# The multiplications of a level half a step after its exponentials, in the recurrence of a two-block kernel

## The chip, the cores and the metric

One NeuronCore of a Trainium2 chip runs the whole program. The time is device microseconds of one execution; before the change three runs gave 2949.8, 2950.39 and 2955.82 us, median 2950.39. The engines are named as the profile names them: PE (TensorE, matrix products; PEld its weight loads), DVE (VectorE), ACT (ScalarE), POOL (GpSimd), SP (SyncE, which here only issues DMAs). Each engine works off its own instructions strictly in order; semaphores make one wait for another.

## What is computed

Two transformer blocks on 512 latent tokens of 1024 features. The change lies in the first block, in a gated linear recurrence (HGRN) with eight heads of 128 features, run forwards and backwards over the tokens. For one direction and chunks of 128 tokens it is

```
def step(s, blk):
    qc, lfc, kc, vc = blk
    b = jnp.cumsum(lfc, axis=2)
    decay = jnp.exp(jnp.where(lower, b[:, :, :, None, :] - b[:, :, None, :, :], -jnp.inf))
    a = jnp.einsum('bhtd,bhsd,bhtsd->bhts', qc, kc, decay)
    o = jnp.einsum('bhts,bhse->bhte', a, vc) + jnp.einsum('bhtd,bhde->bhte', qc * jnp.exp(b), s)
    b_last = b[:, :, -1:, :]
    s_new = jnp.exp(b_last)[:, :, 0, :, None] * s + jnp.einsum('bhsd,bhse->bhde', kc * jnp.exp(b_last - b), vc)
    return s_new, o
```

`log_f` and `k` are the logarithms of a sigmoid of one projection and of its complement. The outputs of both directions are added, normed over the 128 features (`o * rsqrt(mean(o*o) + eps)`), scaled and multiplied with `silu` of another projection. The rest of the block (a gated convolution, grouped attention, a merge, sixteen experts) and the second block are the same before and after.

## The kernel before

Features stand on the partitions, tokens along the free dimension. For each head j a generator `mixer_in` (L628) makes eight products of the 512 latents with a slab of 128 weight columns, four of them with the context's 256 tokens too, and what follows from them alone: the gates of both directions (`lf`, `az`, running sums `P`), the query `q`, the output gate `g`, the values `v` and the convolution `cv`, `b`. A product is 24 matmuls (three for each of 8 k tiles, since each operand is split into two float32r parts) or 48. ACT makes the high part of a weight slab (`whi<-raw`, L153), POOL the low part (`wlo<-raw,whi`, L110), eight of each for a head.

A second generator `hgrn_core` (L738) does the recurrence of the head before. The decays between two tokens of a chunk are taken by halves: for each level m in 16, 8, 4, 2, 1 and 32, 64, the tokens of a block of 2m are decayed to its middle. `halves(m)` (L801) writes four differences of the running sums `P` into a tile `dd` of [128, 2, 512] on DVE, and ACT takes the exponential of all of it; then DVE multiplies its first half with the keys `k` and the second with `q`. PE then forms the products of keys and queries: `near(m)` for levels up to 16, `far(m)` for 32 and 64, and DVE and ACT copy what belongs to the level into `a` or `aT`. The states of the chunks are a chain: PE forms `u` from the turned, decayed keys `kt` and the values, ACT copies the first state `S<-u`, and DVE does three `S<-S,eq,u` for each direction. `read` (L855) makes the output `o` and ACT its squares `sq`; `norm` (L865) sums them over the features on PE (`hs`), then ACT takes Ln and Exp and DVE does four operations on `rstd` and `rstd_t` and multiplies `o` with the result to `a`, which SP stores. Both `o` and `hs` lie in the two PSUM banks that `near` and `far` use as well.

The order is written out by hand. `mixers` (L891) runs the generators side by side: of the eight products of a head each is followed by half a step of the recurrence, what frees the product's bank, another half step, and the rest. A head's recurrence begins with the first product of the next head and, in its last four half steps, goes along with the recurrence of the head after it. Since every engine is in order, the place of an instruction in this program decides what it queues behind. Products take PSUM banks in turn, `dd` has three buffers. After the last head the same loop runs with the keys and values of the attention (`attn_kv`, L963) in the place of projections.

Of the kernel before, what the change touches and what calls it, by code (L numbers as in the profile page):

```python
# [20 lines left out]
S = 512  # L21
# [11 lines left out]
def shape_constants():  # L33
    """Tables that follow from the shapes alone."""
# [33 lines left out]
class Flow:  # L68
    """Slabs of 128 weight columns in the order in which the products use them: loads and exact
    splits into two float32r parts run ahead of the products."""  # L70
# [43 lines left out]
    def fill(self, parts=True):  # L114
        """Loads go out as far ahead as there is room; splits follow a call later, so that no
        engine waits for them."""
        n, there = len(self.plan), self.loaded
        more = True
        while more:
            more = False  # L120
            if self.parted < self.loaded and (self.parted < there or self.parted <= self.pos):
                if len(self.parts) < (self.nparts if parts is True else parts):
                    self.part()
                    more = True
            if self.loaded < n and self.loaded - self.parted < self.nraw:
                self.load()
                more = True
# [10 lines left out]
class Kernel:  # L138
# [42 lines left out]
    def banks(self, es, mm, **pools):  # L181
        """PSUM pools of a phase: mm banks for products, the others by name (tiles, banks each)."""
# [14 lines left out]
    def lin(self, slab, outs):  # L197
        """outs: (psum, high parts, low parts) with one [128, n] part for each k tile."""
# [9 lines left out]
    def first_constants(self, pin):  # L208
# [27 lines left out]
        # resets of the running sums: every 128, every 32, at the start  # L236
# [8 lines left out]
    def first_tables(self):  # L245
        """What the shapes give and the start needs."""
# [24 lines left out]
    def vectors(self, pin, name, items):  # L271
        """Vectors of features, brought to [128, n / 128] with the features on the partitions."""
# [47 lines left out]
    def conditions(self, conds):  # L320
        """silu of c, c_ctx and c_2, features on the partitions, in 32 columns for each 128 features"""
# [5 lines left out]
    def first_mods(self, pool, bufs):  # L327
        """Shifts and scales of the first modulation for c, c_ctx and c_2 at once, 128 features of
        both in a step: functions for the load, the products, and the sums over the partitions."""
# [30 lines left out]
    def mod_load(self, pool, tag, bufs, queue):  # L360
        """The next pair of slabs of the modulations."""
# [6 lines left out]
    def modulate(self, pool, n, bufs, bank, cuts=1, late=1):  # L368
        """Modulations of the one condition that is needed, n pairs of slabs: the products on VectorE
        and only the sums over the partitions on TensorE. Returns a function for a step: the  # L370
        products of a pair take as many calls as there are cuts, and with one buffer the load one
        more. late: how many pairs later the sums come."""
# [47 lines left out]
    def gain(self, name, g, mods, chunk, col):  # L420
        """g * (1 + scale) as [128, 8]."""
# [5 lines left out]
    def rstd(self, pool, ps, n=S, tag="rstd", bufs=2):  # L427
        """ps holds -0.5 * mean of squares, the same in all partitions that share a group."""
# [4 lines left out]
    def rstd_in(self, y, t, ps, eps=None):  # L433
        col, eps = (self.eps2, EPS * EPS) if eps else (self.eps, EPS)
        self.act(y, ps, AF.Ln, scale=-2.0, bias=col)
        self.act(y, y, AF.Exp, scale=-0.5)
        self.tt(t, y, y, OP.mult)
# [14 lines left out]
    def tokens_norm(self, pool):  # L452
        """Two tiles of tokens at a time, as they come."""
# [30 lines left out]
    def tokens_turned(self, k, pool, P):  # L484
        """features k on the partitions, latents and context side by side"""
# [9 lines left out]
    def split(self, pool, src, n=S, tag="h", bufs=None, e=("act", "pool")):  # L495
        """Exact float32r parts of src."""
# [7 lines left out]
    def tokens_modulated(self, k, xn, ph, phc, pool):  # L504
        """h of the latents and of the context, features k, in two parts"""
# [15 lines left out]
    def start(self, ph, phc, pin, P):  # L521
        """The normed and modulated inputs, 128 features at a time as their modulations come, and
        with them the first three products."""
# [26 lines left out]
        def products(end):  # L550
            """with the features up to end"""
# [53 lines left out]
    def softplus(self, a, z):  # L605
        """a = log(1 + exp(-|z|))"""
# [12 lines left out]
    def wide_product(self, key, P):  # L619
        """of the latents and of the context, side by side"""  # L620
# [7 lines left out]
    def mixer_in(self, j, P, st, b_out):  # L628
        """Projections of head j and of convolution channels j, and what follows from them alone:
        eight steps, each a product, what frees its bank, and the rest."""  # L630
# [97 lines left out]
    def transposed(self, src, dst, n, e="act"):  # L728
        """n blocks of 128 columns of src, transposed into dst[:, i, :]."""
# [8 lines left out]
    def hgrn_core(self, h, P, st, a_out):  # L738
        """The recurrence of head h in both directions: within chunks of 128 by halves, from the
        largest to the smallest, so that no exponent is above zero; across chunks by states."""  # L740
# [15 lines left out]
        def decays(d):  # L756
# [9 lines left out]
            else:  # L766
# [4 lines left out]
                self.act(w[:, 3 * C:], px, AF.Exp)  # L771
            self.tt(w[:, 0:3 * C], w[:, 0:3 * C], kk[:, d, d * C:(d + 3) * C], OP.mult)
# [23 lines left out]
        def pairs(*ms):  # L796
            """keys and queries of the two halves of each block of 2m, decayed to the middle."""
            for f in [halves(m) for m in ms]:
                f()

        def halves(m):  # L801
# [11 lines left out]
            self.act(x, x, AF.Exp)  # L813
            both = bass.AP(tensor=kk.tensor, offset=kk.offset,
                           ap=[list(kk.ap[0]), [2 * m, nb], [S + CTX + m, 2], [1, m]])

            def scaled():
                self.tt(dk, dk, both, OP.mult)
                self.tt(x[:, 1, :], x[:, 1, :], q, OP.mult)
            return scaled  # L820
# [43 lines left out]

        def norm():  # L865
            ps = gram(S, "hs")
            self.mm(ps, self.mean[128], st["sq"])
            y = self.rstd(p, ps, bufs=1)
# [4 lines left out]

        steps = [
            (lambda: (key_sum(), decays(0), decays(1), pairs(16)), lambda: (turn(0), diagonal())),
            (lambda: (queries(0), queries(1), pairs(8)), lambda: (states(0), turn(1))),
            (None, lambda: (states(1), near(16), near(8))),
            (lambda: pairs(4, 2), lambda: near(4)),
            (lambda: pairs(1), lambda: near(2)),
            (lambda: pairs(32), lambda: near(1)),  # L880
            (lambda: pairs(64), lambda: far(32)),
            (place, lambda: far(64)),
            (None, read),
            (None, norm)]
        for a, b in steps:
            for f in (a, b):
                if f:
                    f()
                yield

    def mixers(self, P):  # L891
        """HGRN and convolution of all channels: a and b, features on the partitions. Each head's
        recurrence goes along with the next head's projections, the last one's with the keys and
        values of the attention."""
        a = self.pd.tile([8, 128, S], F32, name="a_dram")
        b = self.pd.tile([8, 128, S], F32, name="b_dram")
        with ExitStack() as es:
            P["p"] = self.pool(es, "hgrn")
            cores, st = [], None
            for j in range(10):  # L900
# [6 lines left out]
                for k in range(8):  # L907
# [5 lines left out]
                    if k == 1 and j >= 2:  # L913
                        cores.pop(0)
# [1769 lines left out]
```

## Time and profile before

| | |
|---|---|
| runs | 2949.8, 2950.39, 2955.82 us |
| span of the profiled execution, first to last instruction | 2949.0 us |
| median of the runs less that span | 1.4 us |
| busy in the span | PE 92%, DVE 60%, ACT 37%, POOL 22% |
| recurrence and projections (eight heads) | about 100 to 660 us of the span |
| one head of it | 68.24 us: PE busy 65.58, DVE 54.05, ACT 35.55, POOL 20.29 |
| granted TensorE clock there | 1.00, the higher of its levels, 2.4 GHz |

The profiled execution has no separate time of its own; its span is 0.8 us below the fastest run. A row of the timeline gives when a piece of work began, how long it took, the engine, the line, the operation with what it writes and reads, and in brackets how long the engine had been idle and which engine's instruction ended that. A count such as x4 means that rows of the same kind were merged; the time is then that of all of them. Matmuls overlap, so their durations are longer than the distance from one to the next. The line of most operations is that of a helper (L161 is the DVE's two-operand operation, L158 ACT's function), so groups are told apart by the names of what they write and read.

### The profile page before, as it was taken

What the parts mean: (1) busy time and instruction counts of PE and PEld (TensorE: products, weight loads), DVE (VectorE), ACT (ScalarE), POOL (GpSimd) and SP (SyncE); (2) the same over time, 40 slices, a digit from 0 to 9 for tenths busy, and PEclk for the clock granted to TensorE, in tenths of its full rate; (3) what the DMA queues carried; (4) which work ended last, traced back from release to release, by engine and by line L of the source; (5) the groups of instructions that cost most, each with busy time, mean ns of one, the idle gap of its engine ahead of it and who ended that gap; (6) DMA issues with size and microseconds to landing.
All of it is one profiled execution on the core that took longest, in us unless ns stands there. A gap on an engine that the chain in (4) does not pass through costs nothing.

```text
span 2949.0 us, 39097 instructions
## 1 busy us (share of the span) xinstructions
PE 2727.2 (92%) x15570; PEld 2007.9 (68%) x15570; DVE 1783.2 (60%) x2980; ACT 1087.5 (37%) x1902; POOL 660.4 (22%) x325
## 2 busy tenths in 40 slices
PE   6999999998889998799999889988998998999998
PEld 5878788887667876543333246776777876688887
DVE  6677777767877767712212346577667469553343
ACT  5455555544126653300000035523223246442232
POOL 2222332223333213200000001223443444200000
PEclk9999999999999999899999999999999999999999
DMA  8222222238641115889999961244555521123332
GB/s 236 69 72 65 72 65 83 65 101 268 214 134 40 37 55 173 313 337 409 409 409 408 409 189 40 66 147 149 180 174 152 160 79 37 58 86 100 93 100 79
DMA packets 479028, 466.93 MB, mean 158 GB/s; under 512 B 17757, under 2 KB 421246, under 8 KB 478846
## 3 DMA queue, kind: packets, MB, share of 16 engines
q1 hardware_dynamic: 468494, 453.87, 46.2%
q10 hardware_dynamic: 10352, 10.55, 1.2%
q8 instruction: 123, 2.02, 0.3%
q14 instruction: 59, 0.48, 0.1%
HBM read 452.85 MB, written 11.53 MB: 157 GB/s over the span
## 4 chain that ended last, share of the span: by engine, by line
PE 54%; DVE 27%; ACT 8%; DMA 5%; issue 3%; POOL 0%; SPq 0%; ACTq 0%; DVEq 0%; POOLq 0%
PE mm L173 25%; PE gu L173 6%; DVE modsum L170 5%; DVE dd L161 5%; PE y L173 2%; PE o L173 2%; PE z L173 2%; PE sc L173 2%; DMA ew<-in_w_up_dram 2%; DMA ew<-in_w_gate_dram 2%; PE gate L173 2%; PE proj L173 1%; PE scatter L173 1%; ACT dd L158 1%; DVE modsum L165 1%
## 5 line engine op out<-in xcount | busy, mean ns | idle before, releaser
L110 POOL TENSOR_TENSOR wlo<-raw,whi 128x1024 fp32r<-128x1024 f32 (+2 forms) x249 | 579.6, 2330 | 1784.8 <-ACT whi L153 1267.0
L153 ACT ACTIVATE whi<-raw 128x1024 fp32r<-128x1024 f32 (+2 forms) x322 | 320.8, 1000 | 258.8 <-PE mm L173 170.4
L170 DVE SCALAR_TENSOR_TENSOR modsum<-modw,cs,modsum 128x256 f32<-128x256 f32 x448 | 340.8, 761 | 15.0
L173 PE MATMUL mm<-hi,whi 128*128 128x512 f32 (+1 forms) x676 | 262.0, 388 | 1.2 <-ACT hi L153 1.2
L173 PE MATMUL mm<-lo,whi 128*128 128x512 f32 (+1 forms) x676 | 258.2, 382 | 0.4 <-DVE lo L161 0.4
L173 PE MATMUL mm<-hi,wlo 128*128 128x512 f32 (+1 forms) x676 | 257.7, 381 | 0.0
L173 PE MATMUL gu<-ew,xs 128*64 128x512 f32 x1024 | 239.2, 601 | 9.3 <-DMA ew<-in_w_up_dram 7.0
L173 PEld LDWEIGHTS gu<-ew,xs 128*64 128x64 f32 x1024 | 65.9, 136 | 148.0 <-issue 111.9
L173 PEld LDWEIGHTS mm<-hi,whi 128*128 128x128 f32 x676 | 128.0, 189 | 27.8 <-issue 3.2
L173 PEld LDWEIGHTS mm<-hi,wlo 128*128 128x128 f32 x676 | 127.9, 189 | 24.4
L173 PEld LDWEIGHTS mm<-lo,whi 128*128 128x128 f32 x676 | 128.0, 189 | 24.2 <-DVE lo L161 1.4
L110 DVE TENSOR_TENSOR wlo<-raw,whi 128x1024 fp32r<-128x1024 f32 (+2 forms) x73 | 86.2, 1184 | 77.1 <-ACT whi L153 76.3
L173 PE MATMUL y<-ew,hidT 128*64 128x512 f32 (+1 forms) x576 | 117.9, 550 | 8.3 <-DMA ew<-in_w_down_dram 6.3
L161 DVE TENSOR_TENSOR dd<-P 128x256 f32<-128x256 f32 x224 | 116.3, 583 | 0.0
L170 DVE SCALAR_TENSOR_TENSOR res<-scatter,mods,res 128x512 f32<-128x512 f32 x64 | 48.0, 751 | 102.5 <-PE scatter L173 102.5
L158 ACT ACTIVATE dd<-dd 128x1024 f32<-128x1024 f32 x56 | 59.3, 1058 | 133.1 <-DVE dd L161 133.1
L165 DVE TENSOR_SCALAR e<-e,m 128x768 f32<-128x768 f32 (+4 forms) x160 | 95.1, 611 | 4.5
L158 ACT ACTIVATE relu<-mm 128x512 f32<-128x512 f32 x58 | 34.5, 596 | 163.2 <-PE mm L173 163.2
L173 PE MATMUL mod<-mean,modsum 128*128 128x128 f32 x256 | 43.4, 293 | 55.3 <-DVE modsum L170 55.3
L173 PEld LDWEIGHTS y<-ew,hidT 128*64 128x64 f32 x576 | 39.7, 136 | 74.8 <-issue 50.8
L161 DVE TENSOR_TENSOR relu<-relu 128x512 f32<-128x512 f32 x64 | 45.0, 703 | 74.5 <-ACT relu L158 74.5
L161 DVE TENSOR_TENSOR dd<-dd,k 128x512 f32<-128x512 f32 x56 | 59.7, 1065 | 49.9 <-ACT dd L158 49.9
(1222 smaller groups left out, 6696.8 us busy)
## 6 DMA issues: line engine op xcount, KB each, us to landing
ew<-in_w_gate_dram SPq DMA_DIRECT2D x64, 1024.0 KB
ew<-in_w_up_dram SPq DMA_DIRECT2D x64, 1024.0 KB
raw<-in_w_ff_dram SPq DMA_DIRECT2D x128, 512.0 KB
ew<-in_w_down_dram SPq DMA_DIRECT2D x56, 1024.0 KB
raw<-in_w_in_dram SPq DMA_DIRECT2D x100, 512.0 KB
modw<-in_w_ada_dram SPq DMA_DIRECT2D x48, 1024.0 KB
modw<-in_ada_w_dram SPq DMA_DIRECT2D x16, 1024.0 KB
modw<-in_ada_w_dram SPq DMA_DIRECT2D x16, 512.0 KB
```

The costliest lines, as they stand in the source:

```text
L110: k.eng(f).tensor_tensor(lo, t, hi.bitcast(F32), op=OP.subtract)
L153: self.nc.scalar.activation(out, in_, AF.Copy)
L158: self.nc.scalar.activation(out, in_, func, **kw)
L161: self.eng(e).tensor_tensor(out, a, b, op=op)
L165: self.eng(e).tensor_scalar(out, a, s1, None, op0=op0)
L170: self.nc.vector.scalar_tensor_tensor(out, a, s, b, op0=op0, op1=op1)
L173: self.nc.tensor.matmul(out, lhsT, rhs, start=start, stop=stop, skip_group_check=True)
```

## The change

`halves(m)` now ends with the exponential, and a new `pairs(m)` holds the two products; the half steps of `hgrn_core` are listed anew, with `halves` of a level in one half step and `pairs` in the next. The products of the keys' decays (`keys`) are split from `decays` in the same way. The norm's sum, Ln and Exp (`squares`) stay in the half step where the norm was; its DVE operations and the store come one half step later, so that there are 21 half steps instead of 20, and a head is dropped from the loop one product later. Since the tile `rstd` is now held over a half step, the keys' norm in `attn_kv` uses the tiles `cv` and `q`.

```
+        def keys(d):
+            w = kd[d]
             self.tt(w[:, 0:3 * C], w[:, 0:3 * C], kk[:, d, d * C:(d + 3) * C], OP.mult)
             self.tt(w[:, 3 * C:], w[:, 3 * C:], kk[:, d, S:], OP.mult)
...
-        def pairs(*ms):
-            for f in [halves(m) for m in ms]:
-                f()
-
         def halves(m):
...
             self.act(x, x, AF.Exp)
+
+        def pairs(m):
+            x = X[m]
+            nb = S // (2 * m)
+            dk = x[:, 0, :].rearrange("p (n h j) -> p n h j", h=2, j=m)
             both = bass.AP(tensor=kk.tensor, offset=kk.offset,
                            ap=[list(kk.ap[0]), [2 * m, nb], [S + CTX + m, 2], [1, m]])
-            def scaled():
-                self.tt(dk, dk, both, OP.mult)
-                self.tt(x[:, 1, :], x[:, 1, :], q, OP.mult)
-            return scaled
+            self.tt(dk, dk, both, OP.mult)
+            self.tt(x[:, 1, :], x[:, 1, :], q, OP.mult)
...
+        def squares():
+            ps = st["hs"] = gram(S, "hs")
+            self.mm(ps, self.mean[128], st["sq"])
+            y = st["y"] = p.tile([128, S], F32, tag="rstd", name="rstd", bufs=1)
+            self.act(y, ps, AF.Ln, scale=-2.0, bias=self.eps)
+            self.act(y, y, AF.Exp, scale=-0.5)
+
         def norm():
-            ps = gram(S, "hs")
-            self.mm(ps, self.mean[128], st["sq"])
-            y = self.rstd(p, ps, bufs=1)
+            y = self.rstd_last(st["y"], p.tile([128, S], F32, tag="rstdt", name="rstd_t", bufs=1), st["hs"], EPS)
...
         steps = [
-            (lambda: (key_sum(), decays(0), decays(1), pairs(16)), lambda: (turn(0), diagonal())),
-            (lambda: (queries(0), queries(1), pairs(8)), lambda: (states(0), turn(1))),
-            (None, lambda: (states(1), near(16), near(8))),
-            (lambda: pairs(4, 2), lambda: near(4)),
-            (lambda: pairs(1), lambda: near(2)),
-            (lambda: pairs(32), lambda: near(1)),
-            (lambda: pairs(64), lambda: far(32)),
-            (place, lambda: far(64)),
-            (None, read),
-            (None, norm)]
+            lambda: (decays(0), key_sum(), halves(16), keys(0), decays(1)),
+            lambda: (turn(0), diagonal(), keys(1), pairs(16)),
+            lambda: (queries(0), queries(1), halves(8)),
+            lambda: (states(0), turn(1), pairs(8)),
+            lambda: halves(4),
+            lambda: (states(1), near(16), near(8), pairs(4)),
+            lambda: halves(2),
+            lambda: (near(4), pairs(2)),
+            lambda: halves(1),
+            lambda: (near(2), pairs(1)),
+            lambda: halves(32),
+            lambda: (near(1), pairs(32)),
+            lambda: halves(64),
+            lambda: (far(32), pairs(64)),
+            place, lambda: far(64), None, read, None, squares, norm]
...
-                    if k == 1 and j >= 2:
+                    if k == 2 and j >= 2:
```

How it moves instructions, at three places of a round. On DVE around the norm, before (`lf` and `az` are the next head's gate, `S` the chain of states, x2 two alike):

```order
L170 SCALAR_TENSOR_TENSOR lf<-z,az 128x768
L161 TENSOR_TENSOR az<-lf,z 128x768 [waits DVE_49]
L161 TENSOR_TENSOR rstd_t<-rstd 128x512 [waits Activation_49]
L170 SCALAR_TENSOR_TENSOR rstd_t<-hs,rstd_t 128x512 [waits DVE_49]
L170 SCALAR_TENSOR_TENSOR rstd<-rstd_t,rstd 128x512 [waits DVE_49]
L161 TENSOR_TENSOR rstd<-rstd,g 128x512 [waits DVE_49]
L161 TENSOR_TENSOR a<-o,rstd 128x512 [waits DMAHW4_49,DVE_49,PE_49]
L170 SCALAR_TENSOR_TENSOR S<-S,eq,u 128x128 [waits Activation_49]
L170 SCALAR_TENSOR_TENSOR S<-S,eq,u 128x128 [waits DVE_49] x2
L170 SCALAR_TENSOR_TENSOR S<-S,eq,u 128x128 [waits Activation_49]
L170 SCALAR_TENSOR_TENSOR S<-S,eq,u 128x128 [waits DVE_49] x2
```

The same place after (the two products `dd` are those of level 8, the four differences those of level 4):

```order
L161 TENSOR_TENSOR az<-lf,z 128x768 [waits DVE_49]
L170 SCALAR_TENSOR_TENSOR S<-S,eq,u 128x128 [waits Activation_49]
L170 SCALAR_TENSOR_TENSOR S<-S,eq,u 128x128 [waits DVE_49] x2
L161 TENSOR_TENSOR dd<-dd,k 128x512
L161 TENSOR_TENSOR dd<-dd,q 128x512
L161 TENSOR_TENSOR rstd_t<-rstd 128x512
L170 SCALAR_TENSOR_TENSOR rstd_t<-hs,rstd_t 128x512 [waits DVE_49]
L170 SCALAR_TENSOR_TENSOR rstd<-rstd_t,rstd 128x512 [waits DVE_49]
L161 TENSOR_TENSOR rstd<-rstd,g 128x512 [waits DVE_49]
L161 TENSOR_TENSOR a<-o,rstd 128x512 [waits DMAHW5_49,DVE_49]
L161 TENSOR_TENSOR dd<-P 128x64x4 x4
L170 SCALAR_TENSOR_TENSOR S<-S,eq,u 128x128 [waits Activation_49]
```

The first chain of states and the products of level 8 moved ahead of the norm, and the differences of level 4 ahead of the second chain. On ACT at that place, before and then after (`whi<-raw` makes a slab's high part, `dd<-dd` a level's exponential):

```order
L153 ACTIVATE S<-u 128x128 [waits PE_49]
L153 ACTIVATE kt<-tr 128x512 [waits PE_49]
L153 ACTIVATE kt<-tr 128x128 [waits PE_49]
L153 ACTIVATE whi<-raw 128x1024 [waits DMAHW6_49,Pool_49]
L158 ACTIVATE q<-q 128x512 [waits PE_49]
L153 ACTIVATE S<-u 128x128 [waits PE_49]
L153 ACTIVATE whi<-raw 128x1024 [waits DMAHW0_49,Pool_49]
L158 ACTIVATE dd<-dd 128x1024 [waits DVE_49]
```

After:

```order
L153 ACTIVATE S<-u 128x128 [waits PE_49]
L153 ACTIVATE kt<-tr 128x512 [waits PE_49]
L153 ACTIVATE kt<-tr 128x128 [waits PE_49]
L153 ACTIVATE whi<-raw 128x1024 [waits DMAHW6_49,Pool_49]
L158 ACTIVATE dd<-dd 128x1024 [waits DVE_49]
L158 ACTIVATE q<-q 128x512 [waits PE_49]
L153 ACTIVATE S<-u 128x128 [waits PE_49]
L153 ACTIVATE whi<-raw 128x1024 [waits DMAHW0_49,Pool_49]
```

The exponential of level 4 moved ahead of the copies of `q` and of the second start `S<-u`. The third place is DVE at the end of a head's levels; before, from the output gate `g` on (`dd<-P 128x4x64` are the differences of level 64):

```order
L170 SCALAR_TENSOR_TENSOR g<-g,vec_224,ag 128x512 [waits Activation_49]
L161 TENSOR_TENSOR dd<-P 128x4x64 x4
L161 TENSOR_TENSOR dd<-dd,k 128x512 [waits Activation_49]
L161 TENSOR_TENSOR dd<-dd,q 128x512
L155 COPY aT<-far 32x4x32 [waits PE_49]
L155 COPY aT<-far 32x4x32 [waits Activation_49]
L155 COPY aT<-a_3032 32x4x32 x2
L161 TENSOR_TENSOR b<-cv,u_3593 128x512 [waits DMAHW1_49,PE_49]
```

After, from the differences on:

```order
L161 TENSOR_TENSOR dd<-P 128x4x64 x4
L155 COPY aT<-far 32x4x32 [waits PE_49]
L155 COPY aT<-far 32x4x32 [waits Activation_49]
L161 TENSOR_TENSOR dd<-dd,k 128x512 [waits DVE_49]
L161 TENSOR_TENSOR dd<-dd,q 128x512
L155 COPY aT<-a_3032 32x4x32 x2
L161 TENSOR_TENSOR b<-cv,u_3593 128x512 [waits DMAHW1_49,PE_49]
```

The two products of level 64 moved behind the copies of level 32, the second of which waits for ACT. On ACT the order there is the same before and after: the exponential of level 64, `it<-z`, two `aT<-far`, `whi<-raw`.

## Rows read from the trace of the kernel before

**Rows 1.** Busy time in one round: us, then PE, PEld, DVE, ACT, POOL, clock, DMA.

```profile
394.55:462.79 68.24, 65.58 (x536) 55.47 (x535) 54.05 (x94) 35.55 (x57) 20.29 (x9) 1.00 0.24 70
```

**Rows 2.** Timeline of PE, this round and the last `far`: start, duration, work, idle before.

```profile
398.14 0.46 PE L173 MATMUL near<-dd 128*32 128x32 f32 x32 [0.90 <-DVE a L161]
...
436.49 1.13 PE L173 MATMUL far<-dd 128*128 128x128 f32 x8 [1.38 <-DVE dd L161]
...
438.03 0.47 PE L173 MATMUL z<-h0h,whi 128*128 128x512 f32 x1
...
455.80 1.02 PE L173 MATMUL hs<-sq,mean 128*128 128x512 f32 x2
...
646.22 1.13 PE L173 MATMUL far<-dd 128*128 128x128 f32 x8 [0.16 <-DVE dd L161]
```

**Rows 3.** Waits of PE from 150 to 800 us: total us, times, longest.

```profile
PE far L173 <- DVE dd L161: 10.1, 8, 1.7
...
PE near L173 <- DVE a L161: 6.1, 6, 1.6
...
PE near L173 <- DVE dd L161: 2.4, 6, 0.4
```

**Rows 4.** Waits in this round: total us, times, longest.

```profile
DVE dd L161 <- ACT dd L158: 6.2, 5, 1.6
DVE kd L161 <- ACT kd L158: 3.9, 2, 3.7
...
DVE rstd_t L161 <- ACT rstd L158: 2.2, 1, 2.2
```

**Rows 5.** Timeline of DVE in this round.

```profile
393.82 0.69 DVE L170 SCALAR_TENSOR_TENSOR rstd<-rstd_t,rstd 128x512 f32<-128x512 f32 x1
...
397.40 0.69 DVE L161 TENSOR_TENSOR a<-o,rstd 128x512 f32<-128x512 f32 x1
398.00 2.13 DVE L170 SCALAR_TENSOR_TENSOR S<-S,eq,u 128x128 f32<-128x128 f32 x6
...
408.83 1.42 DVE L161 TENSOR_TENSOR dd<-P 128x256 f32<-128x256 f32 x4
411.87 2.18 DVE L161 TENSOR_TENSOR dd<-dd,k 128x512 f32<-128x512 f32 x1 [1.61 <-ACT dd L158]
...
419.21 3.62 DVE L161 TENSOR_TENSOR dd<-P 128x256 f32<-128x256 f32 x4
...
430.31 3.62 DVE L161 TENSOR_TENSOR dd<-P 128x256 f32<-128x256 f32 x4
435.06 0.69 DVE L161 TENSOR_TENSOR dd<-dd,k 128x512 f32<-128x512 f32 x1 [1.13 <-ACT dd L158]
...
436.87 0.29 DVE L155 COPY aT<-far 32x128 f32<-32x128 f32 x1 [0.33 <-ACT aT L153]
```

**Rows 6.** Timeline of POOL in this round.

```profile
394.18 2.57 POOL L110 TENSOR_TENSOR wlo<-raw,whi 128x1024 fp32r<-128x1024 f32 x1 [6.98 <-ACT whi L153]
398.19 2.40 POOL L110 TENSOR_TENSOR wlo<-raw,whi 128x1024 fp32r<-128x1024 f32 x1 [1.44 <-ACT whi L153]
...
419.04 2.51 POOL L110 TENSOR_TENSOR wlo<-raw,whi 128x1024 fp32r<-128x1024 f32 x1 [5.68 <-ACT whi L153]
```

**Rows 7.** Timeline of ACT in this round.

```profile
395.78 0.60 ACT L158 ACTIVATE q<-q 128x512 f32<-128x512 f32 x1 [1.67 <-PE q L173]
396.89 0.28 ACT L153 ACTIVATE S<-u 128x128 f32<-128x128 f32 x1 [0.52 <-PE u L173]
...
409.84 1.04 ACT L153 ACTIVATE whi<-raw 128x1024 fp32r<-128x1024 f32 x1
...
433.96 1.06 ACT L158 ACTIVATE dd<-dd 128x1024 f32<-128x1024 f32 x1 [3.41 <-DVE dd L161]
434.93 0.79 ACT L158 ACTIVATE it<-z 128x768 f32<-128x768 f32 x1
...
459.24 0.67 ACT L158 ACTIVATE rstd<-hs,cols 128x512 f32<-128x512 f32 x1
```

More of the change, by code (lines that the diff above doesn't have):

```diff
@@ L436, in rstd_in, with rstd_last @@
         self.act(y, y, AF.Exp, scale=-0.5)
+        return self.rstd_last(y, t, ps, eps)
+    def rstd_last(self, y, t, ps, eps):
         self.tt(t, y, y, OP.mult)
@@ L874, in hgrn_core @@
         steps = [
-            (lambda: (key_sum(), decays(0), decays(1), pairs(16)), lambda: (turn(0), diagonal())),
-            (lambda: (queries(0), queries(1), pairs(8)), lambda: (states(0), turn(1))),
-            (None, lambda: (states(1), near(16), near(8))),
-            (lambda: pairs(4, 2), lambda: near(4)),
-            (lambda: pairs(1), lambda: near(2)),
-            (lambda: pairs(32), lambda: near(1)),
-            (lambda: pairs(64), lambda: far(32)),
-            (place, lambda: far(64)),
-            (None, read),
-            (None, norm)]
[L885 to L889, printed above, removed]
+            lambda: (decays(0), key_sum(), halves(16), keys(0), decays(1)),
[12 more added lines that the diff above has]
+            lambda: (far(32), pairs(64)),
+            place,
+            lambda: far(64),
+            None,
+            read,
+            None,
+            squares,
+            norm]
+        for f in steps:
+            if f:
+                f()
+            yield
     def mixers(self, P):
@@ L985, in norm_k @@
             steps = []
-            for a, b, tags in ((0, S, ("rstd", "rstdt")), (S, N, ("Pc0", "Pc1"))):
+            for a, b, tags in ((0, S, ("cv", "q")), (S, N, ("Pc0", "Pc1"))):
                 st = wide[:, a:b] if i else self.ps(S, "k_st")[:, 0:b - a]
@@ L990, in norm_k @@
             for a, b, tags, st in steps:
-                y, t = (p.tile([128, b - a], F32, tag=x, name="k_" + x, bufs=1 if x[0] == "r" else 2) for x in tags)
+                y, t = (p.tile([128, b - a], F32, tag=x, name="k_" + x, bufs=1 if x == "cv" else 2) for x in tags)
                 y = self.rstd_in(y, t, st)
```

## The prediction

> **What bounds the kernel now.** I read the busy time of each engine in one round of the recurrence first, then who waited for whom in it, then its timeline engine by engine. A round is one head: 68.24 us from one `rstd<-rstd,g` of VectorE (DVE) to the next. In it TensorE (PE) is busy for 65.58 us and DVE for 54.05 [rows 1]. So PE is nearly full, and no change of the waits alone can bring a round under some 65.6 us. The 2.7 us that PE lacks lie at three places, each with DVE as the releaser: 0.90 us before `near` of level 8, which waits until the norm's last product `a` gives back its bank; 1.38 us before `far` of level 64 [rows 2]; and 0.4 us before `near` of level 4. Over the stage they sum to 6.1, 10.1 and 2.4 us [rows 3]. DVE in turn waits for ScalarE (ACT): 6.2 us a round for the exponentials of the levels, 3.9 for those of the keys, 2.2 for those of the norm [rows 4]. These are what the change goes for.
>
> The reader is to see one thing more, which no wait row names: DVE loses about 10 us a round to GpSimd (POOL). Four differences of a level take 1.42 us when alone and 3.62 when a slab split `wlo` begins beside them; a product of 0.69 takes 2.18 [rows 5]. The 2.2 us more at 419.21 are what is left of the `wlo` that began at 419.04 [rows 6]. POOL suffers the same: a `wlo` of 2.40 us shows 2.57 when it begins (394.18) inside a DVE instruction on two SBUF tiles, the norm's `rstd<-rstd_t,rstd` of 393.82 [rows 5, 6]. Six state updates `S`, which read PSUM, ran beside the `wlo` of 398.19 in 2.13 us, 0.35 each, unhindered [rows 5, 6]. So a DVE instruction on two SBUF tiles and a `wlo` exclude each other, each for the whole length of the other, and a `wlo` costs DVE nothing only where DVE waits anyway or works from PSUM. DVE's idle time is partly the shelter of eight `wlo` a round.
>
> **The change, part by part.** No arithmetic goes or comes: per level four differences, one exponential and two products, for the norm the same seven instructions; PE's order in a round stays. What moves is DVE's order and two ACT exponentials. I cut the round at two points that PE waits for: stretch A from the end of `a` (397.40 + 0.69 = 398.09) to `far` of level 64 at 436.49, 38.40 us; stretch B the other 29.84 us [rows 1, 2, 5].
>
> *Stretch A.* Because PE idles 1.38 us at its end for DVE, what DVE loses here PE loses too.
> 1. Three of the six `S` now stand ahead of `a`: 2.13 / 2 = -1.05 us [rows 5].
> 2. The other three stand behind the differences of level 4, and on ACT the copy of their start, `S<-u`, stands behind that level's exponential and the copy of `q`. DVE waits for exponential 1.06, `q` 0.60 and `S` 0.28, less the overlap of ACT's successive instructions: +1.8 us [rows 7]. Before, that copy was over at 397.17, ahead of DVE.
> 3. Waits for exponentials. Gone: 1.61 (level 1) and 1.13 (level 32; the row of level 64 shows the same) [rows 5]. In their place: level 2 and level 32 each have only a masked copy of about 0.2 between differences and products, so 1.06 - 0.21 = 0.85 twice; level 1 has the next head's gate between and waits for nothing. 1.70 - 2.74 = -1.0.
> 4. POOL. Before: 2.18 - 0.69 = 1.5, and 3.62 - 1.42 = 2.2 twice (levels 32 and 64) [rows 5]. After: (a) behind the second `S<-u` ACT makes a `whi` (1.04) [rows 7], and its `wlo` (2.40) ends 3.45 after that copy; three `S` and two masked copies shelter only 1.7 of it, so the products of level 4 are held 1.75. (b) Whether the products of level 1 still meet their `wlo` can't be placed to a microsecond: between 0 and the 1.5 of before. The next head's gate now stands ahead of them on DVE, so most of that `wlo` should be over: 0.5. (c) The `wlo` that held the differences of level 32 now meets the convolution's products on two SBUF tiles: 2.4. (d) The one at level 64 stays: 2.2. 6.85 - 5.9 = +0.95.
> 5. The end. Before: differences of 64, exponential, two products, then `far` 2.4 us after the differences. Now DVE's copies `aT<-far` of level 32 stand between. The second waits for ACT's copy of the same tile [0.33 at 436.87, rows 5], and on ACT that copy stands behind the exponential and `it`. So the products start only after 1.06 + 0.79 (`it`) + 0.29 (DVE's `aT`) and as much for ACT's, and last 1.3: 3.7 us, +1.3 [rows 5, 7].
>
> Sum of A: -1.05 + 1.8 - 1.0 + 0.95 + 1.3 = +2.0 us.
>
> *Stretch B.* PE sets the pace here. From `z` at 438.03 the norm's sum `hs` ends 18.8 us later [rows 2]. ACT then does Ln 0.67, an Exp of about as much and `S<-u` 0.28, so DVE gets its `S` at 20.4 at the earliest [rows 7], or about 0.9 later if the differences of level 8 meet a `wlo` on the way and what hangs on them on ACT is late. DVE's waits for keys, levels 16 and 8 and the norm do go, but they go into waiting for `hs` and `u`. Then three `S` 1.05, the products of level 8 1.3, the norm's four 2.8 and `a` 0.65 follow, and a `wlo` (its `whi` comes two copies of turned keys after `S<-u`) falls among them for 2.4: 8.2 us. `a` ends 28.6 to 29.5 after `z`; before it ended at 398.09 + 68.24 - 438.03 = 28.3. +0.3 to +1.2; I take +0.8. The old order did not have the products of level 8 and `S` ahead of the norm; that is what it costs to let the norm wait a half step.
>
> What the norm's second step queues: behind `a` stand the differences of level 4, so ACT's copies and two `wlo`; nothing on SP is late but `a`'s own store, for which nobody in the round waits.
>
> A round: +2.0 + 0.8 = +2.8. `far` of level 64 comes eight times [rows 3], the last at 646.22 [rows 2]; of the seven rounds between, six are as above: +16.8. In the seventh, beside the attention's keys, PE idles only 0.16 at `far` [rows 2]; step 5 and a queue for the norm are paid there in smaller measure: +2. The first head has no norm before it: +0.3. In all +19. The profiled execution spans 2949.0 us, 1.4 below the median of 2950.39 (runs 2949.8 to 2955.82). 2949.0 + 1.4 + 19 = 2969.5.
>
> Bounds. Low: if the convolution's instructions are not held (step 4c, -2.0) and B costs +0.3, a round costs +0.3 and the whole +3. High: 2.25 + 1.2 a round, and +3 at the end: +24, and a `wlo` more on the way to the keys in some rounds, +5: 2979. For 4c the nearest row is the 2.57 us of the `wlo` at 394.18 [rows 6], where an instruction of that form did exclude POOL; so I take the upper value. Beside it, the Trainium skill ("SBUF — State Buffer", section "Who interferes with whom") says that a tensor_scalar in a two-port mode takes the shared pair as well; the convolution begins with one, and no row here shows it beside a `wlo`. By that page step 4c is 2.4; without it the loss begins one instruction later and is some 0.4 less.
>
> **Rivals.**
> 1. *Faster: DVE gets ahead of PE.* It has 14.2 us of idle time a round [rows 1]. If the separated half steps turn that into lead, and no more `wlo` are met than before, DVE needs 44 + 10 us plus the waits of step 2 and 3, below PE's 65.6, and PE's three waits vanish: 6.1 + 10.1 + 2.4 = 18.6 [rows 3], 2932. It decides at `far` of level 64: DVE must do stretch A in 36.6 us instead of 38.4. For it: the waits named are real. Against it: steps 2, 4 and 5. Chance 0.18, parts of that gain included.
> 2. *No change:* the low bound, 2953: waits and collisions change place and nothing more. Chance 0.12.
> 3. *Forecast:* slower, 2969.5, its own range 2957 to 2979. Chance 0.70.
>
> A measurement of this kernel tells about 0.2% (6 us) from no change. So faster 0.18, same 0.12, slower 0.70. The range that leaves out 2 in 10 goes down into the first rival: 2941 to 2979.
>
> **What would show it.** Right: rounds of 70 to 72 us; PE idle before `far` of level 64 grown from 1.38 to 3 to 4.5 and before `near` of level 8 to 1 to 2; its 0.4 at level 4 gone; DVE waiting about 1.8 us for ACT before the second three `S`; the differences of level 64 still near 3.6 us, the convolution's longer by some 2; DVE busier a round than 54 with the same instructions. Step 5 wrong: products of level 64 starting within 1.3 us of the end of their differences. Step 4 wrong: DVE's busy time a round unchanged. All wrong: rounds near 65.6 with PE waiting for nobody.

## The result, and the profile after

The changed kernel takes 2987.71 us (median of five runs) against 2954.11 on the same chip, 33.6 us more. One of the five, the one with the profile, took 4309.97 us at a granted clock of 0.58 throughout; the other four (2983.13 to 2990.26, median 2985.80) give a ratio of 1.0109 [1.0094, 1.0123] and lie 31.7 us above. The forecast was 2969.5, and 2979 was the end of its range: the direction came out as said, the size did not. What follows is read from a second profiled execution of the changed kernel, span 2978.1 us against 2949.0.

The busy time of each engine over six rounds of the recurrence (from `far` of level 64 to the same six heads on) and over the last one, columns as in [rows 1]; first before:

```profile
161.36:572.95 411.59, 394.01 (x3206) 332.82 (x3207) 326.91 (x562) 213.60 (x342) 121.23 (x48) 1.00 0.24 70
572.95:646.22 73.27, 73.11 (x580) 61.23 (x581) 53.39 (x92) 37.15 (x63) 20.32 (x8) 1.00 0.29 90
```

and after:

```profile
161.61:599.80 438.19, 405.14 (x3207) 343.39 (x3207) 336.17 (x562) 213.41 (x343) 121.22 (x49) 0.97 0.23 66
599.80:679.58 79.78, 75.41 (x580) 62.85 (x581) 55.54 (x92) 36.68 (x64) 20.09 (x9) 0.98 0.27 85
```

The six rounds cost 26.6 us more and the last one 6.5; with 0.25 before the first they make 33.4, of which 4.3 come back behind the recurrence. Now split the 26.6: PE's idle time (span minus busy) went from 17.58 to 33.05, +15.5. The other 11.1 us are PE *busy* longer with the same matmuls (3206 and 3207 in the trace). No matmul was added; the clock column fell from 1.00 to 0.97.

The waits of PE after, 150 to 720 us, answer to [rows 3]:

```profile
PE far L173 <- ACT whi L153: 26.7, 8, 3.9
PE near L173 <- DVE a L161: 11.4, 7, 1.7
PE z L173 <- ACT k_raw L158: 1.7, 1, 1.7
```

Level 64 costs 26.7 instead of 10.1 us and level 8 costs 11.4 instead of 6.1; the wait at level 4 is gone; one at the keys of the attention is new. The timeline of PE in one round (start, duration, work, idle before) shows what [rows 2] show of before:

```profile
379.43 2.05 PE L173 MATMUL far<-dd 128*128 128x128 f32 x8 [3.92 <-ACT whi L153]
...
382.41 0.78 PE L173 MATMUL z<-h0h,whi 128*128 128x512 f32 x1
...
412.76 0.46 PE L173 MATMUL near<-dd 128*32 128x32 f32 x32 [1.69 <-DVE a L161]
```

Beside the wait (1.38 before, 3.92 now) the same eight matmuls take 2.05 us instead of 1.13, and the first of `z` 0.78 instead of 0.47. The windows around it say why (clock is the third number from the end):

```profile
378.00:380.00 2.00, 0.57 (x3) 0.60 (x4) 1.96 (x5) 1.93 (x4) 0.58 (x1) 0.56 0.05 16
380.00:382.00 2.00, 2.00 (x11) 2.00 (x11) 0.84 (x3) 0.04 (x1) 1.86 (x1) 0.50 0.00 0
382.00:384.00 2.00, 2.00 (x8) 1.71 (x7) 1.87 (x5) 1.95 (x4) 0.00 (x0) 0.50 0.33 72
384.00:386.00 2.00, 2.00 (x11) 1.81 (x10) 0.25 (x1) 2.00 (x6) 1.60 (x1) 0.73 0.97 305
386.00:388.00 2.00, 2.00 (x13) 1.73 (x13) 1.56 (x2) 2.00 (x6) 0.81 (x1) 1.00 0.10 31
```

PE stood still for 3.92 us and then got 0.50, the lower of its two levels (1.2 of 2.4 GHz), for 5 to 6 us of its work. In the same place of before, after a wait of 1.4 us, the clock is 1.00 in every window.

The whole stretch from `far` to the end of `a` (stretch B of the prediction), first before, then after:

```profile
436.49:466.32 29.83, 28.98 (x230) 25.08 (x230) 20.55 (x35) 21.00 (x40) 10.31 (x4) 1.00 0.22 63
379.43:412.71 33.28, 31.64 (x230) 27.51 (x230) 21.84 (x35) 17.76 (x34) 10.25 (x4) 0.92 0.25 72
```

The round shown is one of the two worst. Over the six rounds this stretch lasts 31.43, 32.22, 32.15, 33.28, 32.26 and 33.41 us, against 31.74 and then five times 29.8 before.

DVE in that round answers to [rows 5]:

```profile
406.93 2.88 DVE L161 TENSOR_TENSOR rstd_t<-rstd 128x512 f32<-128x512 f32 x1
...
412.02 0.69 DVE L161 TENSOR_TENSOR a<-o,rstd 128x512 f32<-128x512 f32 x1
...
415.82 1.11 DVE L170 SCALAR_TENSOR_TENSOR S<-S,eq,u 128x128 f32<-128x128 f32 x3 [1.78 <-ACT S L153]
417.46 2.30 DVE L161 TENSOR_TENSOR dd<-dd,k 128x512 f32<-128x512 f32 x1
...
425.70 0.69 DVE L161 TENSOR_TENSOR dd<-dd,k 128x512 f32<-128x512 f32 x1 [0.97 <-ACT dd L158]
...
430.95 1.42 DVE L161 TENSOR_TENSOR dd<-dd,k 128x512 f32<-128x512 f32 x1
432.89 2.62 DVE L165 TENSOR_SCALAR cv<-u,vec 128x512 f32<-128x512 f32 x1
...
439.55 0.69 DVE L161 TENSOR_TENSOR dd<-dd,k 128x512 f32<-128x512 f32 x1 [0.91 <-ACT dd L158]
...
445.70 3.62 DVE L161 TENSOR_TENSOR dd<-P 128x256 f32<-128x256 f32 x4
...
451.42 0.29 DVE L155 COPY aT<-far 32x128 f32<-32x128 f32 x1 [1.92 <-ACT aT L153]
451.74 0.69 DVE L161 TENSOR_TENSOR dd<-dd,k 128x512 f32<-128x512 f32 x1
452.35 0.69 DVE L161 TENSOR_TENSOR dd<-dd,q 128x512 f32<-128x512 f32 x1
```

and POOL answers to [rows 6]:

```profile
406.34 2.93 POOL L110 TENSOR_TENSOR wlo<-raw,whi 128x1024 fp32r<-128x1024 f32 x1 [6.11 <-ACT whi L153]
416.81 2.39 POOL L110 TENSOR_TENSOR wlo<-raw,whi 128x1024 fp32r<-128x1024 f32 x1 [7.55 <-ACT whi L153]
...
432.74 2.48 POOL L110 TENSOR_TENSOR wlo<-raw,whi 128x1024 fp32r<-128x1024 f32 x1 [1.07 <-ACT whi L153]
...
446.02 2.67 POOL L110 TENSOR_TENSOR wlo<-raw,whi 128x1024 fp32r<-128x1024 f32 x1 [10.80 <-ACT whi L153]
```

An instruction on two SBUF tiles that is 0.69 alone shows 2.88 (406.93) or 2.30 (417.46) beside a `wlo`, and `cv` shows 2.62 while the `wlo` of 432.74 runs; before, with no `wlo` beside it, it took

```profile
417.25 0.48 DVE L165 TENSOR_SCALAR cv<-u,vec 128x512 f32<-128x512 f32 x1
```

The last four rows of DVE are step 5: from the end of the differences (449.32) to `far` (453.18) it takes 3.86 us, since the products stand behind a copy that waits 1.92 for ACT. On ACT:

```profile
449.35 1.06 ACT L158 ACTIVATE dd<-dd 128x1024 f32<-128x1024 f32 x1 [3.40 <-DVE dd L161]
450.31 0.79 ACT L158 ACTIVATE it<-z 128x768 f32<-128x768 f32 x1
451.12 0.27 ACT L153 ACTIVATE aT<-far 32x128 f32<-32x128 f32 x1
```

### The profile page after: what moved, and what is told of

It reads as the page before. It is cut to its first block, busy times and chain, and to the rows that moved or that the text cites. A ratio compares the mean times of both kernels' runs of the same rounds, so it can differ in the third digit from the quotient of the medians.

```text
span 4308.2 us, 39110 instructions
## 1 busy us (share of the span) xinstructions
PE 4237.1 (98%) x15570; PEld 2485.4 (58%) x15570; DVE 1717.3 (40%) x2980; ACT 1098.4 (25%) x1902; POOL 647.4 (15%) x325
## 4 chain that ended last, share of the span: by engine, by line
PE 97%; DVE 2%; DMA 0%; ACT 0%; issue 0%; SPq 0%; DVEq 0%; ACTq 0%
PE mm L173 32%; PE gu L173 10%; PE z L173 9%; PE u L173 6%; PE gate L173 5%; PE proj L173 5%; PE y L173 5%; PE o L173 4%; PE sc L173 3%; PE g L173 2%; PE tr L1190 2%; PE aq L173 2%; PE q L173 1%; PE mod L173 1%; PE scatter L173 1%; PE f L173 1%
## 5 line engine op out<-in xcount | busy, mean ns | idle before, releaser
L173 PE MATMUL gu<-ew,xs 128*64 128x512 f32 x1024 | 407.3, 963 | 0.0
L173 PE MATMUL mm<-hi,whi 128*128 128x512 f32 (+1 forms) x676 | 352.6, 522 | 0.0
L173 PE MATMUL mm<-lo,whi 128*128 128x512 f32 (+1 forms) x676 | 347.3, 514 | 0.0
L173 PE MATMUL mm<-hi,wlo 128*128 128x512 f32 (+1 forms) x676 | 346.9, 513 | 0.0
L170 DVE SCALAR_TENSOR_TENSOR modsum<-modw,cs,modsum 128x256 f32<-128x256 f32 x448 | 318.1, 710 | 15.1
L173 PE MATMUL y<-ew,hidT 128*64 128x512 f32 (+1 forms) x576 | 202.6, 886 | 0.0
L173 PEld LDWEIGHTS mm<-lo,whi 128*128 128x128 f32 x676 | 146.6, 217 | 76.1 <-issue 32.7
L173 PE MATMUL proj<-hi,whi 128*128 128x512 f32 x192 | 112.9, 588 | 1.2 <-ACT hi L153 1.2
L173 PE MATMUL proj<-lo,whi 128*128 128x512 f32 x192 | 111.1, 579 | 0.3 <-DVE lo L161 0.3
L173 PE MATMUL proj<-hi,wlo 128*128 128x512 f32 x192 | 110.2, 574 | 0.0
L170 DVE SCALAR_TENSOR_TENSOR mods<-mod,vec 128x2 f32<-128x2 f32 x64 | 10.1, 157 | 249.0 <-PE mod L173 248.9
```

The costliest lines, as they stand in the source:

```text
L170: self.nc.vector.scalar_tensor_tensor(out, a, s, b, op0=op0, op1=op1)
L173: self.nc.tensor.matmul(out, lhsT, rhs, start=start, stop=stop, skip_group_check=True)
```

## The experiments

Three theories stand in the expectations. W: only the waits count; PE's added idle time is the loss. C: the clock that falls after those waits costs as much again, as PE time. L: DVE comes late because of `wlo`, and all the rest follows. Ratios are to the kernel before on the same chip, with their interval.

**The changed kernel once more,** with nothing altered.

> The changed kernel once more, for a profile at full clock: the first one was taken with the clock down all through. Theory W (waits alone): granted clock 1.00 in the recurrence, rounds of 72 to 73 us instead of 68.24, PE idle before far of level 64 about 4 us and before near of level 8 about 2. Rival C (clock): rounds of 70 to 71 us where the clock is 1.00, and stretches of the recurrence with a granted clock below 1.00 that make up the rest of the 33 us.

2985.54 us, 1.0104 [1.0089, 1.0119], 30.7 above its before. The rows above are its profile. The waits are about as long as W said, 3.9 and 1.7 us, but the clock that it put at 1.00 is 0.97 over the six rounds; the stretches of low clock that C named are there.

**Level 64's products ahead of the copies again.**

```
-            lambda: (far(32), pairs(64)),
+            lambda: (pairs(64), far(32)),
```

> The changed kernel with the two products of level 64 ahead of the copies of level 32 again (step 5 undone, all else as changed). Theory W: 1.3 us a round, 9 us in all, less than the changed kernel: about 2977. Rival C: the wait before far of level 64 is the longest PE idle of a round, so clock comes back with it: 15 to 25 us less, 2960 to 2970.

2968.53 us, 1.0049 [1.0034, 1.0064]: 17.0 less than the changed kernel. The waits of PE, 150 to 800 us:

```profile
PE far L173 <- DVE dd L161: 17.7, 8, 2.9
PE near L173 <- DVE a L161: 11.1, 7, 1.7
```

The wait at level 64 shrank by 9.0 and the time by 17: C, not W. In the six rounds PE's idle time is 6.8 us less and its busy time 5.1 us less than in the changed kernel. This one line is more than half of the loss.

**The norm in one step again.**

```
-            squares,
-            norm]
+            lambda: (squares(), norm()),
+            None]
```

> The changed kernel with the norm's DVE operations back in the half step of its sum (ahead of the first state updates and the products of level 8). Theory W: the end of a comes about 0.8 us earlier in a round, 5 to 6 us in all: about 2980. Rival C: more, 2965 to 2975, if the wait before near of level 8 was what lowered the clock. If stretch A is the whole loss: no change, 2986.

2982.53 us, 1.0095 [1.008, 1.011]: 3.0 less, and the interval overlaps that of the changed kernel, so no gain is shown. The norm's place alone is worth little; DVE then comes late to levels 8 and 64 by another way (the wait for `far` sums to 27.9 us, that for the products of `near` to 8.9). My 5 to 6 was too much.

**Level 4's differences behind the second state updates again.** The masked copies of levels 16 and 8 still come after them, not before as in the kernel before.

```
-            lambda: halves(4),
-            lambda: (states(1), near(16), near(8), pairs(4)),
+            None,
+            lambda: (states(1), halves(4), near(16), near(8), pairs(4)),
```

> The changed kernel with the differences of level 4 behind the second state updates, so that ACT's copy S<-u is not queued behind that level's exponential (step 2 undone; the exponential of level 4 then has only the masked copies as cover). Theory W: 1.8 us less waiting for S, 0.4 to 0.8 more for the exponential: 1 us a round, 7 us in all, about 2979. Rival: the POOL split shifts with it and eats the gain: 2986.

2975.65 us, 1.0083 [1.0065, 1.01]: 9.9 less by the medians, 6.2 by the ratios, whose intervals overlap; 7 were expected. The wait at `far` is 22.8, and in the profile the six rounds are 5.5 us shorter and the last one 3.8. The three parts, undone one at a time, give 17.0 + 3.0 + 9.9 = 29.9 of 30.7 by the medians, but about 16 + 3 + 6 = 25 by the ratios. They were not undone together.

**PE kept at work through the wait.** Sixteen matmuls without use stand ahead of `far` of level 64, in its bank; they wait for nothing that DVE does late, and `far` overwrites them.

```
             g = gram(S, "far")
+            for _ in range(16 if m == 64 else 0):
+                self.mm(g, self.h[0][0][:, 0:C], self.h[0][1])
```

> The changed kernel with 16 matmuls of 512 columns more before far of level 64, into the bank that far then overwrites: 16 x 0.23 = 3.6 us of PE work that falls into its idle 3.9 us there; DVE, ACT and POOL have the same instructions. Theory C (the idle stretch lowers the granted clock, and that costs the PE time beyond the waits): clock 1.00 in the recurrence, PE's own work back to that of before, 10 to 13 us less than the changed kernel: 2973 to 2976. Rival W (the clock is not what costs; DVE and ACT set the pace through the low stretch too): the same time as the changed kernel, 2986, or a little more.

2976.02 us, 1.0082 [1.0062, 1.0101]; 9.5 less than the changed kernel by the medians, on another chip; by the ratios about 6.5, with overlapping intervals, where 10 to 13 were expected. The profile agrees with the ratios: the six rounds take 431.57 us instead of 438.19. PE, in the round shown above:

```profile
375.69 3.80 PE L173 MATMUL far<-h1h,h0h 128*128 128x512 f32 x16
379.32 1.06 PE L173 MATMUL far<-dd 128*128 128x128 f32 x8
```

and its clock there:

```profile
372.00:376.00 4.00, 4.00 (x19) 3.28 (x19) 3.09 (x4) 1.07 (x2) 2.28 (x1) 1.00 0.12 28
376.00:380.00 4.00, 4.00 (x23) 3.41 (x22) 2.61 (x6) 2.90 (x6) 1.23 (x1) 1.00 0.36 107
380.00:384.00 4.00, 4.00 (x28) 3.61 (x27) 2.68 (x6) 3.08 (x7) 1.90 (x2) 1.00 0.33 81
```

`far` comes no earlier (41.54 us behind `near` of level 8, against 40.43), PE does 3.80 us of useless work, and the rounds are shorter: `far`'s own matmuls are back at 1.06 us and the clock stays at 1.00. This shows the clock's share apart from the wait's. Not all of it came back: low clock now follows the 1.7 us at level 8 in four of the six rounds, where it did in one of the changed kernel.

**No reads by POOL, in both kernels.** The low parts of the slabs that POOL splits during the recurrence are left out: a memset of zeros writes them. It also takes 0.95 us where a `wlo` takes 2.40, so POOL's time goes with its reads.

```
-        k.eng(f).tensor_tensor(lo, t, hi.bitcast(F32), op=OP.subtract)
+        if f == "pool" and getattr(k, "free", False):
+            k.nc.gpsimd.memset(lo.bitcast(F32), 0.0)
+        else:
+            k.eng(f).tensor_tensor(lo, t, hi.bitcast(F32), op=OP.subtract)
```

> The changed kernel, where in the recurrence stage POOL fills the low part of each weight slab with zeros instead of computing it, so that POOL reads no SBUF there (the low parts are left out of the projections' result). Theory L (what holds DVE back is the exclusion by the low-part splits, about 11 us a round after the change): stretch A falls from 40.5 to about 34, below PE's 36.2; rounds of 65.5 to 67 us, 2940 in all. Rival Q (queueing on ACT, the waits for S and aT, holds it back): stretch A still 38 or more, 2970 or more.

> The kernel before with the same zeros in place of the low parts in the recurrence stage. Theory L: its three PE waits go, rounds of 65.5 to 66 us: 2932 to 2936. Rival Q: 2945 or more. Between this run and the changed kernel with zeros, theory L expects a difference of at most 8 us, where the two kernels differ by 31.

The changed order: 2927.08 us, 0.9916 [0.9895, 0.9937]. The old one: 2928.08, 0.9918 [0.9898, 0.9939]. Both have rounds of 65.11 us. Busy time from 200 to 600 us of the changed order:

```profile
200.00:600.00 400.00, 399.00 (x3263) 339.43 (x3262) 265.95 (x564) 215.90 (x350) 45.39 (x48) 1.00 0.25 74
```

and of the old:

```profile
200.00:600.00 400.00, 400.00 (x3268) 340.46 (x3267) 267.27 (x563) 218.01 (x348) 45.72 (x48) 1.00 0.25 74
```

Without the splits' work on POOL the two orders cost the same, and PE is full in both. So the added queues on DVE and ACT alone cost nothing that PE sees; the whole difference of 31 us needs the splits. That is L in part: with the splits in place the queues do count, since one of them, at level 64, was worth 17 us above. The splits take the room that DVE would need for them, and C is how lateness gets its size. This pair of runs takes POOL's reads and most of its time away together; that a split holds DVE up while both want SBUF rests on the rows of DVE beside a `wlo`.

**The exponentials ahead, the products where they were.** If the splits make the harm, a part of the change may still help: in the kernel before, the differences and exponentials of levels 1, 32 and 64 go a half step ahead, and nothing else moves.

```
-            (lambda: pairs(4, 2), lambda: near(4)),
-            (lambda: pairs(1), lambda: near(2)),
-            (lambda: pairs(32), lambda: near(1)),
+            (lambda: (halves(4), halves(2), pairs(4), pairs(2), halves(1)), lambda: near(4)),
+            (lambda: pairs(1), lambda: (near(2), halves(32))),
+            (lambda: pairs(32), lambda: (near(1), halves(64))),
```

> The kernel before with half of the change where the chain of waits has use for it: differences and exponentials of the levels 1, 32 and 64 one half step ahead of their products, the products where they were, the norm and the states as before, products of level 64 ahead of the copies of level 32. If the exponential's wait and the split's exclusion both lie beside other DVE work then, the wait before far of level 64 (1.4 us a round) goes and that before near of level 8 (0.9) stays: 2936 to 2944. If the splits only fall on other instructions: 2950 to 2956.

2949.18 us, 0.9987 [0.9977, 0.9998]; the 2936 to 2944 of the first theory were not reached. The waits at level 64 are gone, 10.1 us, and the time moved by about 4: most of the gain was given back at level 8, where DVE's `a` is late in six rounds (9.8 us instead of 6.1) and a low clock follows in five. In the profile the six rounds take 410.43 us, 1.2 less than before. PE and the clock there:

```profile
259.61 0.46 PE L173 MATMUL near<-dd 128*32 128x32 f32 x32 [1.64 <-DVE a L161]
```

```profile
258.00:260.00 2.00, 0.39 (x32) 0.35 (x32) 1.88 (x4) 0.84 (x1) 1.30 (x2) 1.00 0.03 8
260.00:262.00 2.00, 2.00 (x18) 1.71 (x9) 1.79 (x7) 0.00 (x0) 1.29 (x1) 0.68 0.69 203
262.00:264.00 2.00, 2.00 (x8) 1.71 (x7) 2.00 (x3) 0.00 (x0) 0.00 (x0) 0.50 1.01 278
```

**The same, and the norm's first factor early.** `o` leaves its bank by the gate's product `a = o*g`, before the norm is known; the norm is multiplied in place.

```
-            self.tt(y, y, st["g"], OP.mult)
+            self.tt(a, st["o"], st["g"], OP.mult)
+            y = self.rstd(p, ps, bufs=1)
-            self.tt(a, st["o"], y, OP.mult)
+            self.tt(a, a, y, OP.mult)
```

> The run before (levels 1, 32 and 64 half a step ahead) with the norm's products in another order: o times g first, which gives o's bank back before the norm's factors are there, then times the factor. Theory C and L: PE's last wait of a round (1.6 us before near of level 8) goes, and with it the low clock that followed it; rounds of 65.2 to 66.5 us, 2928 to 2936. Rival: near waits for the sum's bank instead, half of it gone: 2940.

**2942.66 us, 0.9966 [0.9953, 0.9979]: faster than both kernels.** Rounds of 66.60 us; the waits at 64 and 8 are gone, one for the products of level 4 is left, and the clock shows 1.00 from 200 to 600 us:

```profile
PE near L173 <- DVE dd L161: 8.5, 6, 1.4
```

```profile
200.00:600.00 400.00, 392.48 (x3223) 333.95 (x3224) 333.70 (x553) 215.07 (x346) 117.14 (x47) 1.00 0.24 71
```

The 2928 to 2936 that I expected was too good, by that last wait. The norm's last product no longer frees the bank, but it still holds DVE up:

```profile
254.75 2.75 DVE L161 TENSOR_TENSOR a<-a,rstd 128x512 f32<-128x512 f32 x1
```

**The early factor in the changed kernel** (the same edit there).

> The changed kernel with that order of the norm's products. Theory W (DVE's own stretch sets a round, PE waits where DVE comes late): the wait before near of level 8 goes, but DVE comes to far of level 64 at most 0.7 us earlier (one product fewer behind the states), so PE waits there 1 us or more longer: 2980 to 2987, 0 to 5 us less than the changed kernel. Rival: the waits are separate costs, 1.7 us a round and the clock with it: 2965 to 2974.

2978.59 us, 1.0091 [1.0073, 1.0109]; beside the changed kernel's 1.0104 the intervals overlap. The wait for `a` at level 8 is gone, level 4 waits for 2.8 us again, and level 64 pays:

```profile
PE far L173 <- ACT whi L153: 31.5, 8, 4.6
```

DVE late is late at the next place that PE comes to.

**Level 4 ahead too.** To the best version, `halves(4)` goes behind `near(8)`:

```
-            (None, lambda: (states(1), near(16), near(8))),
-            (lambda: (halves(4), halves(2), pairs(4), pairs(2), halves(1)), lambda: near(4)),
+            (None, lambda: (states(1), near(16), near(8), halves(4))),
+            (lambda: (pairs(4), halves(2), halves(1), pairs(2)), lambda: near(4)),
```

> The last faster version (levels 1, 32 and 64 half a step ahead, o times g first), now with the differences and exponential of level 4 one half step ahead too, behind the masked copies of levels 16 and 8, so that the next head's running sums lie between, and those of level 1 between the exponential and the products of level 2. Theory W: the one PE wait that is left in a round (1.4 us before near of level 4) goes: rounds of 65.2 to 65.6 us, 6 to 9 us less, 2934 to 2937 where the kernel before has 2952. Rival: the split's exclusion falls on the products of level 4 then: 2943.

2950.58 us, 1.0 [0.9991, 1.001], where 2934 to 2937 were expected: the gain is gone. The exponential is now ready, and in its place a split meets the product. DVE, then POOL:

```profile
266.71 2.80 DVE L161 TENSOR_TENSOR dd<-dd,k 128x512 f32<-128x512 f32 x1
```

```profile
266.08 2.89 POOL L110 TENSOR_TENSOR wlo<-raw,whi 128x1024 fp32r<-128x1024 f32 x1 [6.66 <-ACT whi L153]
```

PE waits 13.2 us at level 4 instead of 8.5, up to 2.2, and a low clock follows four of these six waits.

## Why the prediction was right and wrong

**Stretch A, +2.0: right, term by term.** In the round shown `a` ends at 412.71 and `far` starts at 453.18: 40.47 us, 38.40 + 2.07. The second `S` waits 1.78 for ACT (1.8 said). The exponentials of levels 2 and 32 are late by 0.97 and 0.91 (0.85 said). Step 4: the first product of level 4 takes 2.30, so it is held 1.61 (1.75 said); that of level 1 is held 0.73 (0.5); `cv` is held 2.62 - 0.48 = 2.1 (2.4); the differences of 64 are at 3.62 as before. Step 5: 3.86 us from differences to `far` (3.7 said), and the wait of 3.9 lies in the 3 to 4.5 named. One reading there was off: before, `far` came 2.56 us after the differences (430.31 + 3.62 to 436.49), not 2.4, so 3.7 would have made +1.1; measured it is +1.3. Stretch A is 40.47 to 40.49 us in five of the rounds and 41.05 in the first: +12.7 over six rounds, where 12.0 were forecast.

**What would show it.** The wait at level 8 grew to 1.7 (1 to 2 said), level 4's 0.4 went, and DVE is busy 336.17 us in six rounds instead of 326.91 with the same instructions. The rounds are 438.19 / 6 = 73.0 us, above the 70 to 72.

**The step that failed: Stretch B's +0.8 in the sum of a round.** The sum was 2.8 us, of waits alone, and the waits did come to about that: 15.5 us more in six rounds where 16.8 were forecast for the whole of them. But PE's work behind a wait was taken at its old duration. That is the +0.8, worked from "`hs` ends 18.8 us after `z`" and from `z` at its old distance from `far`. Over six rounds stretch B grew by 13.9 us where 4.8 were forecast: 3.9 of idle time, and 10.0 in which PE is busy longer. In the round shown, from `far` at 379.43 to the end of `a` at 412.71, it takes 33.28 us, 3.4 more than 29.84. PE's busy time in it went from 28.98 to 31.64, which is the whole excess over the +0.8; `far` takes 0.92 longer and the 48 matmuls of `z` 9.86 instead of 8.65, at the lower clock. Over all six rounds, both stretches, it is the 11.1 us of PE busy time, for which the sum had no term; the filler shows that the clock and not the order of the matmuls makes it. No row of before could have given the price: in its six rounds the clock is 1.00 behind every wait.

**The last round.** Forecast +2, measured +6.5: 4.2 of idle time and 2.3 of busy time. Beside level 8 (1.2 more) and level 64 there was a wait that the prediction did not have, 1.7 us for ACT's copy of the attention's keys, which now stands behind the exponential of level 4. Last comes what wasn't in the sum either way: 4.3 us less behind the recurrence. That stretch takes from 2298.5 to 2310.5 us in the profiles of these experiments, so whether the change does it is open. +16.8, +2, +0.3 became +26.6, +6.5, +0.25, less 4.3: 29.1 between the two spans, where 19 was said.

**The rivals.** DVE did not get ahead of PE. Of the reasons given against it these runs bear out step 4: with the splits' work taken off POOL it does get ahead, in either order, and rounds fall to 65.1, below the 65.6 I gave as PE's floor.

## What to carry to other kernels

Where PE is nearly full, price a new wait of PE twice: its length, and the matmuls behind it at the lower clock; look in the windows of the trace at what the clock did behind waits that are already there. Before filling an engine's idle time, ask who uses that time: here DVE's gaps were the shelter of POOL's splits, and instructions moved into them met those. A wait removed is a gain only when the engine that was late is early at the next place too, so follow it to there.

## What the runs showed of the hardware

- After PE stood still for 3.9 us the granted clock was down for 5 to 6 us of its work in the round shown, and 16 matmuls in the gap kept it at 1.00. After 1.64 us at level 8 it fell in the version with exponentials ahead (259.61), while the same 1.64 us in the kernel before (up to 193.16) left it at 1.00. In the changed kernel 1.70 us there lowered it in one round (193.10) and left it at 1.00 in the other five. What decides is open.
- `cv`, one SBUF operand and a column of scalars, took 2.62 us beside a `wlo` and 0.48 us without one (417.25 of the kernel before). The Trainium skill ("SBUF — State Buffer", section "Who interferes with whom") counts a tensor_scalar in a two-port mode among the instructions that can take the port pair that VectorE shares with GpSimd; these two rows agree.
- A wait row can name a releaser that has nothing to do with the wait: it puts `far` of level 64 down to ACT's `whi`, which `far` does not read. DVE's second product, which it does read, ended at 452.35 + 0.69 = 453.04, 0.14 us before `far`.
